# A state-space branch with its channels on partitions: tiled float32 products and scan rows in another order

## The chip, the cores and the metric

The kernel runs on one core of a Trainium2 chip. The metric is the device time of one execution in microseconds (us), taken as the median of three runs. The engines named below are TensorE (PE, with its weight loads PEld), VectorE (DVE), ScalarE (ACT), GpSimd (POOL) and SyncE (SP, which issues the DMAs here).

## What is computed

One residual block over 256 tokens of width 2048, in float32. One input projection feeds an mLSTM branch, a state-space branch (S5) and two gates; both branches are projected up, gated and added, then come an output projection and a SwiGLU network. The change concerns the S5 branch, which runs once:

```python
step = jnp.exp(log_step.astype(f32))[:, None]
a_bar = jnp.exp(lam * step)
b_bar = ((a_bar - 1.0) / lam)[..., None] * b_mat
ug = uf.reshape(bsz, s, S_GROUPS, S_GROUP).astype(jnp.complex64)   # 32 groups x 16 channels
bu = jnp.einsum('gpc,bsgc->bsgp', b_bar, ug)                       # 64 complex states per group
_, states = lax.associative_scan(linear_recurrence_combine, (a_seq, bu), axis=1)
y = jnp.einsum('gcp,bsgp->bsgc', c_mat, states).real.reshape(bsz, s, S_WIDTH)
y = y + d.astype(f32) * uf
y = jax.nn.gelu(y)
y = y * jax.nn.sigmoid(y @ w_glu.astype(f32) + b_glu.astype(f32))
```

## The kernel before

**The weight stream.** All weights arrive as 427 blocks of 128x1024 float32 on SP's DMA queue. ACT copies a block to `hi` in the rounded type float32r (L156), and DVE subtracts to get the rest `lo` (helper `TT`, L94). With both, each large product is done as three float32r products (`hi` with `hTh`, `lo` with `hTh`, `hi` with `hTl`): a block takes 12 matmuls of 512 columns on PE (`o2_block`, helper `mm`, L100). Three buffers of `hi` and `lo` let the splits run up to two blocks ahead of PE. The blocks come in the order of a table; chunk 4 of the input projection, which makes the S5 input `u`, is first (blocks 0 to 7), then the chunks of `x_m` and others.

**The two chains.** Between the blocks two Python generators are pumped, `s5_gen` for the S5 branch and `ml_gen` for the mLSTM branch. A generator emits a piece and yields its price for DVE and PE; `pump` spends a budget of each per block. A scheduler then reorders what was emitted, so the order on each engine is fixed before the run, and instructions of the chains stand between those of the blocks. The conv of the mLSTM branch is on DVE (`xcT`, `xml`).

**The S5 chain.** Two groups of 64 states fill the 128 partitions; there are 16 such pairs `j`. The input `u` has tokens on partitions (`s5ud`, 2 x 128x512). To bring it under the block-diagonal B, `u` and B are split into three float32r parts (`u`, `s5bd`), turned by products with the identity into `ust` and `bst` (96 rows deep), and 32 products of 256 columns make `bu`. `bu` holds, for each partition, [real or imaginary, pair `j`, token]. The scan runs inside 16 chunks of 16 tokens. Step `tau` makes, for all chunks at once, two products into `stm` (128x512: 2 x 16 pairs x 16 chunks), one addition to `bu` of 128x512 and two of 128x256; there are 15 steps. As a token's chunk is the outer index, a step reads one element, leaves 15 out, and reads the next. A recurrence over the chunks and a correction (`stm`, `bu`, 128x960) follow. Then 64 float32 products of 32 columns (the states as weights, block-diagonal C `cbd` in the tile `s5sp` moving) give `y` with tokens on partitions; after the gelu eight transposes on PE turn it to channels on partitions, in which the GLU product needs it.

Of the kernel before, what the change touches and what calls it, by code (L numbers as in the profile page):

```python
# [29 lines left out]
for _n, _w in (  # L30
    ("gmix", 16), ("g2", 16), ("cw", 32), ("cb", 8), ("mh", 8), ("skip", 8),
    ("bglu", 4), ("bif", 8), ("are", 16), ("aim", 16), ("ls", 16),
):
    PV[_n] = (_o, _o + _w)
    _o += _w
# [12 lines left out]
def block_kernel(ctx: ExitStack, tc: tile.TileContext, d, out):  # L48
# [56 lines left out]
    # ---------------------------------------------------------------- constants  # L105
# [19 lines left out]
    # ---------------------------------------------------------------- weight stream  # L125
# [114 lines left out]
    # ---------------------------------------------------------------- small helpers  # L240
# [29 lines left out]
    # ---------------------------------------------------------------- S5 chain  # L270
    s5 = {}

    def s5_gen():
# [5 lines left out]
        bd = [t2([P, 16, 32]) for _ in range(2)]  # L279
# [4 lines left out]
        nc.gpsimd.memset(bd[0], 0.0)  # L284
        nc.gpsimd.memset(bd[1], 0.0)
# [63 lines left out]
        while "bc" not in s5:  # L349
            yield 0  # L350
        bc = s5["bc"]
        bx = lambda a, n=16: a.unsqueeze(2).broadcast_to([P, 16, n])
        ta = m2([P, 16, 16])
        tb = m2([P, 16, 16])
        bdr = [u8([P, 16, 96], F32R, name="s5bd") for _ in range(2)]
        for ri in range(2):
            TT(ta, bc[:, 0 if ri == 0 else 1], bx(fr), MUL)
            TT(tb, bc[:, 1 if ri == 0 else 0], bx(fi), MUL)
            for g in range(2):
                ps_ = slice(g * 64, g * 64 + 64)  # L360
                TT(bd[ri][ps_, :, g * 16 : g * 16 + 16], ta[ps_], tb[ps_], SUB if ri == 0 else ADD)
            bv = bdr[ri].rearrange("p j (r c) -> p j r c", r=3)
            A.copy(bv[:, :, 0, :], bd[ri])
            A.copy(bv[:, :, 1, :], bd[ri])
            TT(bv[:, :, 2, :], bd[ri], f(bv[:, :, 0, :]), SUB)
            yield 1.8
        for g in range(2):
            ps_ = slice(g * 64, g * 64 + 64)
            cs = slice(g * 16, g * 16 + 16)
            V.tensor_copy(cbd[ps_, :, 0, cs], bc[ps_, 2])  # L370
            TS(cbd[ps_, :, 1, cs], bc[ps_, 3], -1.0)
        yield 1.0
        state["bd"] = 1
        yield 0.01, 0, 1
        # block-diagonal B, stacked (hi, hi, lo) along the contraction rows
        bst = [u8([P, 8, 2, 128], F32R, name="bst") for _ in range(2)]
        for jp in range(8):
            ps_ = aux()
            for jj in range(2):
                for ri in range(2):  # L380
                    c = (jj * 2 + ri) * 128
                    mm(ps_[0:96, c : c + 128], bdr[ri][:, 2 * jp + jj, :], identr, True, True)
            o = bst[jp // 4][:, 2 * (jp % 4) : 2 * (jp % 4) + 2].rearrange("p a b c -> p (a b c)")
            A.copy(o[0:96], ps_[0:96])
            yield 0.05, 0.45, (jp % 4) // 3
        state["bst"] = 1
        while "u" not in state:
            yield 0
        yield 0.01, 0, 2
        u3 = s5["u3"]  # L390
        bu = u32([P, 2, 16, 256], name="bu")
        usts = []
        for h in range(2):
            ust = u8([P, 8, 256], F32R, name="ust")
            usts.append(ust)
            for jp in range(4 * h, 4 * h + 4):
                ps_ = aux()
                for jj in range(2):
                    for tt in range(2):
                        c = (jj * 2 + tt) * 128  # L400
                        mm(ps_[0:96, c : c + 128], u3[tt][:, 2 * jp + jj, :], identr, True, True)
                o = ust[:, 2 * (jp % 4) : 2 * (jp % 4) + 2].rearrange("p a b -> p (a b)")
                A.copy(o[0:96], ps_[0:96])
                yield 0.05, 0.45, (jp % 4) // 3
        yield 0.01, 0, 1
        for h in range(2):
            ust = usts[h]
            for j in range(8 * h, 8 * h + 8):
                ps_ = aux()
                for ri in range(2):  # L410
                    mm(
                        ps_[:, ri * 256 : ri * 256 + 256],
                        bst[h][0:96, j % 8, ri, :],
                        ust[0:96, j % 8, :],
                        True,
                        True,
                    )
                A.copy(bu[:, :, j, :], ps_.rearrange("p (r t) -> p r t", r=2))
                yield 0.05, 0.25, (j % 3) // 2
        state["bu"] = 1  # L420
        # powers of a_bar: pw[:, ri, j, n] = a^(n+1)
# [18 lines left out]
        # scan inside chunks of 16  # L440
        X = bu.rearrange("p r j (c q) -> p r j c q", q=16)
        bc2 = lambda a: a.unsqueeze(1).unsqueeze(3).broadcast_to([P, 2, 16, 16])
        stm = u8([P, 2, 1024], name="stm")
        for tau in range(1, 16):
            pr = X[:, :, :, :, tau - 1]
            cu = X[:, :, :, :, tau]
            ta, tb = (stm[:, k, 0:512].rearrange("p (r j c) -> p r j c", r=2, j=16) for k in range(2))
            TT(ta, pr, bc2(ar), MUL)
            TT(tb, pr, bc2(ai), MUL)
            yield 1.2  # L450
            TT(cu, cu, ta, ADD)
            TT(cu[:, 0], cu[:, 0], tb[:, 1], SUB)
            TT(cu[:, 1], cu[:, 1], tb[:, 0], ADD)
            yield 1.3
        state["scan"] = 1
        # chunk-level recurrence
        for ri in range(2):
            V.tensor_copy(E[:, ri], X[:, ri, :, :, 15])
# [13 lines left out]
        # states: chunk-local + a^(tau+1) * state at the end of the chunk before; y = Re(C s) + D u, gelu  # L472
        ud = s5["ud"]

        def y_mm(jq, half):
            if half == 0:
                s5["yps"] = aux()
            ps_ = s5["yps"]
            for j in range(4 * jq + 2 * half, 4 * jq + 2 * half + 2):
                for tt in range(2):  # L480
                    c = tt * 256 + (j % 4) * 32
                    for ri in range(2):
                        mm(
                            ps_[:, c : c + 32],
                            bu[:, ri, j, tt * 128 : tt * 128 + 128],
                            cbd[:, j, ri, :],
                            ri == 0,
                            ri == 1,
                        )
            if half:  # L490
                pv_ = ps_.rearrange("p (a b) -> p a b", a=2)[:, :, 0:128]
                yv = ud[:, :, jq * 128 : jq * 128 + 128]
                TT(yv, pv_, yv, ADD)

        def gelu(h):
            y = ud[:, :, h * 256 : h * 256 + 256]
# [6 lines left out]
            A.activation(y, t, AF.Copy, scale=0.5)  # L503

        for jq in range(4):
            js = slice(4 * jq, 4 * jq + 4)
            sh = [P, 4, 15, 16]
            pb = [pw[:, ri, js, :].unsqueeze(2).broadcast_to(sh) for ri in range(2)]
            eb = [E[:, ri, js, 0:15].unsqueeze(3).broadcast_to(sh) for ri in range(2)]
            ta, tb = (stm[:, k, 0:960].rearrange("p (j c q) -> p j c q", j=4, c=15) for k in range(2))  # L510
            o = [X[:, ri, js, 1:16, :] for ri in range(2)]
            for ri in range(2):
# [6 lines left out]
                if jq and not ri:  # L519
                    y_mm(jq - 1, 0)  # L520
                    yield 0.05, 1.7
                    y_mm(jq - 1, 1)
                    yield 0.35, 1.7
# [5 lines left out]
        y_mm(3, 0)  # L529
        yield 0.05, 1.7  # L530
        y_mm(3, 1)
        yield 0.35, 1.7
        gelu(1)
        yield 1.9, 0, 1
        yt = u32([P, 2, 4, 256], name="yt")
        ygT = yt[:, 0]
        s5["sgt"] = yt[:, 1]
        ghl = u8([P, 2, 4, 256], F32R, name="ghl")
        gh, gl = ghl[:, 0], ghl[:, 1]
        for cpair in range(2):  # L540
            ps_ = aux()
            for cc in range(2):
                for tt in range(2):
                    ct = 2 * cpair + cc
                    c = (cc * 2 + tt) * 128
                    PE.transpose(ps_[:, c : c + 128], s5["ud"][:, tt, ct * 128 : ct * 128 + 128], ident)
            sl = slice(2 * cpair, 2 * cpair + 2)
            v2 = lambda a: a[:, sl, :].rearrange("p a b -> p (a b)")
            A.copy(v2(ygT), ps_)
            A.copy(v2(gh), v2(ygT))  # L550
            TT(v2(gl), v2(ygT), f(v2(gh)), SUB)
            yield 0.6, 0.45, 0
# [15 lines left out]
    # ---------------------------------------------------------------- mLSTM chain  # L568
    ml = {}

    def ml_gen():
# [93 lines left out]
        # log sigmoid of the forget gate  # L665
# [158 lines left out]
    # ---------------------------------------------------------------- main stream  # L824
# [9 lines left out]
    def win_evac(n, acc):  # L834
        if n == 4:
            u3 = u16([P, 2, 16, 96], F32R, name="u3")
            s5["u3"] = [u3[:, 0], u3[:, 1]]
            db = t2()
            nc.sync.dma_start(db, d["dbc"])
            ud = cp.tile([P, 2, 512], F32, name="s5ud")  # L840
            s5["ud"] = ud
            for tt in range(2):
                uf = ud[:, tt]
# [526 lines left out]
```

## Time and profile before

| what | value |
|---|---|
| median of 3 runs | 1292.4 us (1292.08 to 1292.52) |
| span of the profiled execution, first to last instruction | 1291.1 us |
| PE busy | 1264.4 us, 98% |
| DVE busy | 808.5 us, 63% |
| ACT busy | 611.8 us, 47% |
| chain that ended last | PE 85%, DVE 11%, issue 2% |

The profiled execution has no time of its own beside its span; 1.3 us lie between the span and the median. Busy is an average over the whole span: PE is near its full span, and DVE has three tenths free overall, but not in each stretch.

### The profile page before, as it was taken

The page shows a single profiled execution, that of the slowest core. Times are in us where ns is not written, and L with a number is a line of the kernel's source. Part 1 is how long each engine was busy: PE and PEld are TensorE (multiplying, and loading weights), DVE is VectorE, ACT ScalarE, POOL GpSimd, SP SyncE. Part 2 cuts the span into 40 slices and gives each one's busy share as a digit, 9 for nine tenths or more (in the row PEclk, how much of TensorE's full clock was granted, in tenths as well). Part 3 has the DMA queues.
Part 4 walks back from the last instruction along what each step waited for, and adds up shares of the span by engine and source line. Part 5 has one row for each costly group of instructions (what it writes and reads, how often), then busy time and mean ns, then how long its engine had stood idle before and what let it go on. Part 6 is the DMA issues. An engine that isn't in the chain of part 4 may idle for free.

```text
span 1291.1 us, 15585 instructions
## 1 busy us (share of the span) xinstructions
PE 1264.4 (98%) x5932; PEld 1053.8 (82%) x5932; DVE 808.5 (63%) x1127; ACT 611.8 (47%) x768; POOL 2.1 (0%) x8
## 2 busy tenths in 40 slices
PE   7999989999999999999999999999999999999997
PEld 5888877888888888888888888888888888888885
DVE  8848996899958665565555545555555554545544
ACT  6777533354655445454444444444444433434443
POOL 0000000000000000000000000000000000000000
PEclk9999998999999999999999999999999999999999
DMA  7655445444445576665556665455655666666454
GB/s 273 209 167 171 159 146 166 161 159 136 147 145 174 183 246 191 241 226 186 194 190 186 188 193 188 147 170 189 205 186 163 208 240 195 201 188 203 151 164 145
DMA packets 66874, 238.23 MB, mean 185 GB/s; under 512 B 7408, under 2 KB 8176, under 8 KB 66544
## 3 DMA queue, kind: packets, MB, share of 16 engines
q1 hardware_dynamic: 66800, 237.25, 56.5%
q8 instruction: 46, 0.75, 0.2%
q14 instruction: 28, 0.23, 0.1%
HBM read 235.12 MB, written 2.10 MB: 184 GB/s over the span
## 4 chain that ended last, share of the span: by engine, by line
PE 85%; DVE 11%; issue 2%; ACT 1%; DMA 0%; SPq 0%; ACTq 0%; DVEq 0%
PE acc L100 80%; PE aux L100 4%; DVE lo L94 3%; DVE bu L94 2%; DVE stm L94 2%; PE aux L1097 1%; DVE s5sp L94 0%; DMA raw<-in_w_in_dram 0%; ACT hi L156 0%; DVE hTl L97 0%; DVE xcT L97 0%; DVE m L97 0%; PE aux L1036 0%; PE aux L1000 0%; PE aux L808 0%
## 5 line engine op out<-in xcount | busy, mean ns | idle before, releaser
L94 DVE TENSOR_TENSOR lo<-raw,hi 128x1024 fp32r<-128x1024 f32 x427 | 522.9, 1225 | 427.9 <-ACT hi L156 425.9
L156 ACT CAST hi<-raw 128x1024 fp32r<-128x1024 f32 x427 | 449.4, 1053 | 598.9 <-PE acc L100 522.7
L100 PE MATMUL acc<-lo,h2h 128*128 128x512 f32 x704 | 275.0, 391 | 0.0
L100 PE MATMUL acc<-hi,h2l 128*128 128x512 f32 x704 | 274.0, 389 | 0.0
L100 PE MATMUL acc<-hi,h2h 128*128 128x512 f32 x704 | 249.9, 391 | 0.0
L100 PE MATMUL acc<-hi,aT 128*128 128x512 f32 x664 | 204.9, 389 | 0.0
L100 PE MATMUL acc<-lo,hTh 128*128 128x512 f32 x416 | 168.4, 405 | 5.7 <-DVE lo L94 5.5
L100 PE MATMUL acc<-hi,hTl 128*128 128x512 f32 x416 | 165.2, 397 | 0.0
L100 PE MATMUL acc<-hi,hTh 128*128 128x512 f32 x416 | 154.6, 399 | 9.3 <-ACT hi L156 9.3
L100 PEld LDWEIGHTS acc<-hi,h2h 128*128 128x128 f32 x704 | 132.1, 188 | 27.2
L100 PEld LDWEIGHTS acc<-lo,h2h 128*128 128x128 f32 x704 | 132.1, 188 | 27.1
L100 PEld LDWEIGHTS acc<-hi,h2l 128*128 128x128 f32 x704 | 132.2, 188 | 27.1
L100 PEld LDWEIGHTS acc<-hi,aT 128*128 128x128 f32 x664 | 124.6, 188 | 25.8
L100 PE MATMUL acc<-lo,aT 128*128 128x512 f32 x332 | 129.2, 389 | 0.0
L100 PEld LDWEIGHTS acc<-hi,hTh 128*128 128x128 f32 x416 | 78.8, 191 | 25.6 <-ACT hi L156 9.7
L100 PEld LDWEIGHTS acc<-lo,hTh 128*128 128x128 f32 x416 | 79.6, 191 | 24.7 <-DVE lo L94 9.3
L100 PEld LDWEIGHTS acc<-hi,hTl 128*128 128x128 f32 x416 | 79.5, 191 | 15.5
L100 PEld LDWEIGHTS acc<-lo,aT 128*128 128x128 f32 x332 | 62.3, 188 | 12.9
L94 DVE TENSOR_TENSOR bu<-bu,stm 128x256 f32<-128x256 f32 (+2 forms) x61 | 52.4, 881 | 0.1
L100 PE MATMUL acc<-lo,mTh 128*128 128x512 f32 x128 | 50.2, 392 | 0.0
L100 PE MATMUL acc<-hi,mTl 128*128 128x512 f32 x128 | 49.8, 389 | 0.0
L100 PE MATMUL acc<-hi,mTh 128*128 128x512 f32 x128 | 46.0, 391 | 0.0
(251 smaller groups left out, 982.5 us busy)
## 6 DMA issues: line engine op xcount, KB each, us to landing
raw<-in_w_in_dram SPq DMA_DIRECT2D x104, 512.0 KB, 3.6
raw<-in_w_ffn_gate_dram SPq DMA_DIRECT2D x88, 512.0 KB, 3.5
raw<-in_w_ffn_up_dram SPq DMA_DIRECT2D x88, 512.0 KB, 3.5
raw<-in_w_ffn_down_dram SPq DMA_DIRECT2D x88, 512.0 KB, 4.3
raw<-in_w_out_dram SPq DMA_DIRECT2D x32, 512.0 KB, 3.6
raw<-in_w_up_m_dram SPq DMA_DIRECT2D x16, 512.0 KB, 3.9
raw<-in_w_up_s_dram SPq DMA_DIRECT2D x8, 512.0 KB, 3.5
t<-in_bg_dram SPq DMA_DIRECT2D x8, 256.0 KB, 3.5
```

The costliest lines, as they stand in the source:

```text
L94: return V.tensor_tensor(o, a, b, op=op)
L100: return PE.matmul(o, l, r, start=start, stop=stop, skip_group_check=True)
L156: A.copy(hi, raw)
L1097: PE.transpose(ps_[:, (cc * 2 + tt) * 128 : (cc * 2 + tt) * 128 + 128], av[tt][:, ct * 128 : ct * 128 + 128], ident,)
```

## The change

Chunk 4 is multiplied the other way round, with the weights stationary and the tokens moving, so that `u` leaves PE with channels on partitions; its eight blocks take 192 products of 256 columns instead of 96 of 512. Its evacuation multiplies by the reciprocal norm of a token, which is now needed along the columns: a product with ones spreads it over the partitions (`r1b`). `u` goes straight into tiled float32 products: B in the tile `s5bT` is taken 32 rows at a time as weights, each with 32 channel rows of `u`, and the four strips of rows write four PSUM tiles. The identity products, the splits of `u` and B, `bst` and `ust` are gone. Per token order, `bu` is now [position in chunk, chunk], so that a scan step reads rows of 16 neighbours. The products with C take `cbd` as weights, 32 columns wide, and write 32 PSUM rows each, so that `y` is made with channels on partitions; the eight transposes and the copies behind them are gone. The factor of the ZOH step is applied to C and not to B, D u is added in the evacuation of `y`, and the last copy of the gelu puts the tokens back in order. Two constants are loaded ahead of their old place and one is gone; the first blocks' DMA queue has 0.5 MB more on it.

```diff
-        for h in range(2):
-            ust = usts[h]
-            for j in range(8 * h, 8 * h + 8):
-                ps_ = aux()
-                for ri in range(2):
-                    mm(
-                        ps_[:, ri * 256 : ri * 256 + 256],
-                        bst[h][0:96, j % 8, ri, :],
-                        ust[0:96, j % 8, :],
...
+        for ct in range(4):
+            pss = [aux() for _ in range(4)]
+            for ri in range(2):
+                for jj in range(4):
+                    rs = slice(32 * jj, 32 * jj + 32)
+                    mm(pss[jj][:, ri * 256 : ri * 256 + 256], bT[rs, ct, ri, :], uT[rs, ct, :], True, True)
+            for jj in range(4):
+                A.copy(bu[:, :, 4 * ct + jj, :], pss[jj].rearrange("p (r t) -> p r t", r=2))
+            yield 0.05, 1.3, 1
...
-        X = bu.rearrange("p r j (c q) -> p r j c q", q=16)
+
+        X = bu.rearrange("p r j (q c) -> p r j q c", c=16)
...
-            pr = X[:, :, :, :, tau - 1]
-            cu = X[:, :, :, :, tau]
+            pr = X[:, :, :, tau - 1, :]
+            cu = X[:, :, :, tau, :]
...
+        def y_mm(jq):
+            ps_ = aux()
+            for ri in range(2):
+                for jj in range(4):
+                    j = 4 * jq + jj
+                    mm(ps_[32 * jj : 32 * jj + 32, 0:256], cbd[:, j, ri, :], bu[:, ri, j, :], ri == 0, ri == 1)
+            STT(ud[:, jq, :], ud[:, jq, :], pvs("s5d", jq), ps_[:, 0:256], MUL, ADD)
...
+            rb = s5["r1b"].rearrange("p (q c) -> p q c", c=16).unsqueeze(1).broadcast_to([P, 2, 16, 16])
+            for h in range(2):
+                o = ud[:, 2 * h : 2 * h + 2, :].rearrange("p a (q c) -> p a q c", c=16)
+                TT(o, acc[h].rearrange("p (a c q) -> p a q c", a=2, q=16), rb, MUL)
...
+                for ct in range(4):
+                    mm(o_(ct), w_(hi, ct), xh, kt == 0 and ct % 2 == 0, False)
+                    mm(o_(ct), w_(hi, ct), xl, False, False)
+                for ct in range(4):
+                    mm(o_(ct), w_(lo, ct), xh, False, kt == 15 and ct % 2 == 1)
```

On PE, where the states' input is made, the kernel before has these rows; `aux` is a PSUM tile, and `x2` is the real and the imaginary product of one pair.

```order
L100 MATMUL acc_683<-hi_804,hTh_77 128x512
L100 MATMUL aux_838<-ust_734,bst_606 128x256 x2
L100 MATMUL acc_683<-lo_805,hTh_77 128x512
L100 MATMUL acc_683<-hi_804,hTl_79 128x512
L100 MATMUL aux_842<-ust_734,bst_606 128x256 x2
```

In the changed kernel the second of its four sets of tiled products stands in the stream like this; aux_701, 702, 703 and 704 are the strips of rows 0, 32, 64 and 96.

```order
L100 MATMUL acc_761<-hi_685,hTh_76 128x512
L100 MATMUL aux_701<-s5ud,s5bT_400 128x256
L100 MATMUL aux_702<-s5ud,s5bT_400 128x256
L100 MATMUL aux_701<-s5ud,s5bT_400 128x256
L100 MATMUL aux_703<-s5ud,s5bT_400 128x256
L100 MATMUL aux_704<-s5ud,s5bT_400 128x256
L100 MATMUL aux_702<-s5ud,s5bT_400 128x256
L100 MATMUL aux_703<-s5ud,s5bT_400 128x256
L100 MATMUL aux_704<-s5ud,s5bT_400 128x256
L100 MATMUL acc_761<-lo_686,hTh_76 128x512
```

The eight products of a set stand as neighbours, mostly on different strips, between two products of the stream that use the whole array.

On DVE, the scan of the kernel before stands among the splits `lo` like this; one step is `stm` x2, `bu` of 512 and `bu` of 256 x2.

```order
L94 TENSOR_TENSOR stm_1428<-bu_733,s5sm 128x512 x2
L94 TENSOR_TENSOR bu_733<-bu_733,stm_1428 128x512
L94 TENSOR_TENSOR lo_1503<-raw_1408,hi_1502 128x1024
L94 TENSOR_TENSOR bu_733<-bu_733,stm_1428 128x256 x2
L94 TENSOR_TENSOR stm_1428<-bu_733,s5sm 128x512 x2
L94 TENSOR_TENSOR bu_733<-bu_733,stm_1428 128x512
L94 TENSOR_TENSOR lo_1535<-raw_1431,hi_1534 128x1024
```

In the changed kernel the scan begins at block 20 instead of block 42; these rows are at blocks 25 to 27 (`lo_934` is the split of block 25).

```order
L94 TENSOR_TENSOR lo_934<-raw_874,hi_933 128x1024
L97 SCALAR_TENSOR_TENSOR xcT_1016<-xmT_1015,pv,xcT_1016 128x254 x2
L94 TENSOR_TENSOR stm_928<-bu_666,s5sm 128x512 x2
L94 TENSOR_TENSOR lo_957<-raw_892,hi_956 128x1024
L94 TENSOR_TENSOR xcT_1016<-xcT_1016,m_1570 128x512
L97 SCALAR_TENSOR_TENSOR xcT_1016<-xmT_1015,pv,xcT_1016 128x255 x2
L94 TENSOR_TENSOR bu_666<-bu_666,stm_928 128x32x16
L94 TENSOR_TENSOR lo_979<-raw_910,hi_978 128x1024
L94 TENSOR_TENSOR xml_1227<-xmT_1015,xmh_1226 128x1024
L97 SCALAR_TENSOR_TENSOR xcT_1016<-xmT_1015,pv,xcT_1016 128x253 x4
L94 TENSOR_TENSOR bu_666<-bu_666,stm_928 128x16x16 x2
L94 TENSOR_TENSOR xml_1227<-xmT_1015,xmh_1226 128x1024
```

The scan's rows have moved to where the conv of the mLSTM branch also stands, and out of the later blocks.

## Rows read from the trace of the kernel before

**Rows 1.** Page, busy time and the chain that ended last, by engine.
```profile
PE 1264.4 (98%) x5932; PEld 1053.8 (82%) x5932; DVE 808.5 (63%) x1127; ACT 611.8 (47%) x768; POOL 2.1 (0%) x8
...
PE 85%; DVE 11%; issue 2%; ACT 1%; DMA 0%; SPq 0%; ACTq 0%; DVEq 0%
```

**Rows 2.** PE timeline, 166 to 209 us: start, length, instruction, idle before and releaser.
```profile
166.19 0.50 PE L100 MATMUL acc<-lo,hTh 128*128 128x512 f32 x1 [1.19 <-DVE lo L94]
...
171.29 0.38 PE L100 MATMUL aux<-xch,lo 128*128 128x256 f32 x1 [2.05 <-DVE lo L94]
...
175.53 0.38 PE L100 MATMUL aux<-xch,lo 128*128 128x256 f32 x1 [1.11 <-DVE lo L94]
...
202.07 0.79 PE L100 MATMUL acc<-lo,hTh 128*128 128x512 f32 x1 [3.09 <-DVE lo L94]
...
203.09 0.63 PE L100 MATMUL acc<-lo,hTh 128*128 128x512 f32 x1
203.52 0.63 PE L100 MATMUL acc<-hi,hTl 128*128 128x512 f32 x1
...
208.19 0.39 PE L100 MATMUL acc<-lo,hTh 128*128 128x512 f32 x1
```

**Rows 3.** Windows: length, busy time of PE, PEld, DVE, ACT, POOL, granted clock, DMA.
```profile
180.00:202.00 22.00, 18.98 (x97) 15.59 (x95) 21.86 (x26) 7.96 (x9) 0.00 (x0) 0.98 0.48 144
202.00:209.00 7.00, 6.92 (x18) 5.47 (x19) 4.50 (x6) 1.04 (x1) 0.00 (x0) 0.56 0.67 219
```

**Rows 4.** Chain of waits in order of time: start, length, instructions.
```profile
60.39 1.34 PE aux L100 x16
...
134.22 5.75 PE aux L100 x48
...
329.44 1.71 PE aux L100 x16
...
603.62 43.34 PE acc L100 x191
```

**Rows 5.** Groups of instructions on PE, by form: busy time, mean ns.
```profile
L100 PE MATMUL aux<-s5sp,bu 128*128 128x32 f32 x128 | 15.3, 267 | 0.0
L100 PE MATMUL aux<-ust,bst 96*128 96x256 f32 x32 | 5.9, 285 | 0.0
...
L100 PE MATMUL aux<-identr,u 128*96 128x128 f32 x32 | 3.1, 246 | 0.0
```

**Rows 6.** PE timeline, 313 to 317 us: float32 products.
```profile
313.93 2.75 PE L100 MATMUL aux<-vk,m 128*128 128x256 f32 x12
316.51 0.75 PE L100 MATMUL aux<-s5sp,bu 128*128 128x32 f32 x6
```

**Rows 7.** Groups of instructions on DVE, by form.
```profile
L94 DVE TENSOR_TENSOR stm<-bu,s5sm 128x512 f32<-128x512 f32 x30 | 30.0, 1042 | 0.3
...
L94 DVE TENSOR_TENSOR bu<-bu,stm 128x256 f32<-128x256 f32 x30 | 17.2, 619 | 0.1
L94 DVE TENSOR_TENSOR bu<-bu,stm 128x512 f32<-128x512 f32 x15 | 16.4, 1091 | 0.0
...
L94 DVE TENSOR_TENSOR xcT<-xcT,m 128x512 f32<-128x512 f32 x4 | 2.8, 690 | 0.9 <-ACT m L646 0.9
...
L94 DVE TENSOR_TENSOR m<-s5bc,s5sm 128x256 f32<-128x256 f32 x4 | 1.6, 421 | 0.0
```

**Rows 8.** DVE timeline, 106 to 110 us, in the conv.
```profile
106.43 0.48 DVE L97 SCALAR_TENSOR_TENSOR xcT<-xmT,pv,xcT 128x255 f32<-128x255 f32 x1
106.82 0.69 DVE L94 TENSOR_TENSOR xcT<-xcT,m 128x512 f32<-128x512 f32 x1
107.42 0.48 DVE L97 SCALAR_TENSOR_TENSOR xcT<-xmT,pv,xcT 128x255 f32<-128x255 f32 x1
107.82 1.22 DVE L94 TENSOR_TENSOR xml<-xmT,xmh 128x1024 fp32r<-128x1024 f32 x1
108.95 1.23 DVE L94 TENSOR_TENSOR lo<-raw,hi 128x1024 fp32r<-128x1024 f32 x1
```

More of the change, by code (lines that the diff above doesn't have):

```diff
@@ L31 @@
     ("gmix", 16), ("g2", 16), ("cw", 32), ("cb", 8), ("mh", 8), ("skip", 8),
-    ("bglu", 4), ("bif", 8), ("are", 16), ("aim", 16), ("ls", 16),
+    ("bglu", 4), ("s5d", 4), ("bif", 8), ("are", 16), ("aim", 16), ("ls", 16),
 ):
@@ L278, in s5_gen @@
         ar, ai, fr, fi, am1, inv = (sv(i) for i in range(13, 19))
-        bd = [t2([P, 16, 32]) for _ in range(2)]
         sp = u8([P, 2048], name="s5sp")
@@ L283, in s5_gen @@
         cbd = sp[:, 1024:2048].rearrange("p (a b c) -> p a b c", a=16, b=2)
-        nc.gpsimd.memset(bd[0], 0.0)
-        nc.gpsimd.memset(bd[1], 0.0)
         nc.gpsimd.memset(cbd, 0.0)
@@ L348, in s5_gen @@
         yield 1.0
-        while "bc" not in s5:
+        while "cc" not in s5:
             yield 0
-        bc = s5["bc"]
-        bx = lambda a, n=16: a.unsqueeze(2).broadcast_to([P, 16, n])
+        cc_ = s5["cc"]
+        bx = lambda a: a.unsqueeze(2).broadcast_to([P, 16, 16])
         ta = m2([P, 16, 16])
         tb = m2([P, 16, 16])
-        bdr = [u8([P, 16, 96], F32R, name="s5bd") for _ in range(2)]
         for ri in range(2):
-            TT(ta, bc[:, 0 if ri == 0 else 1], bx(fr), MUL)
-            TT(tb, bc[:, 1 if ri == 0 else 0], bx(fi), MUL)
+            TT(ta, cc_[:, ri], bx(fr), MUL)
+            TT(tb, cc_[:, 1 - ri], bx(fi), MUL)
@@ L359, in s5_gen @@
             for g in range(2):
                 ps_ = slice(g * 64, g * 64 + 64)
[L361 to L377, printed above, removed]
-            ps_ = aux()
-            for jj in range(2):
-                for ri in range(2):
[L381 to L385, printed above, removed]
@@ L386, in s5_gen @@
-        state["bst"] = 1
+                o = cbd[ps_, :, ri, g * 16 : g * 16 + 16]
+                if ri == 0:
+                    TT(o, ta[ps_], tb[ps_], SUB)
+                else:
+                    STT(o, ta[ps_], -1.0, tb[ps_], MUL, SUB)
+            yield 1.6
+        state["cbd"] = 1
         while "u" not in state:
             yield 0
-        yield 0.01, 0, 2
-        u3 = s5["u3"]
+        yield 0.01, 0, 1
+        uT = s5["ud"]
+        bT = s5["bT"]
         bu = u32([P, 2, 16, 256], name="bu")
-        usts = []
@@ L393, in s5_gen @@
-        for h in range(2):
[L394 to L404, printed above, removed]
@@ L405, in s5_gen @@
-        yield 0.01, 0, 1
-        for h in range(2):
-            ust = usts[h]
-            for j in range(8 * h, 8 * h + 8):
-                ps_ = aux()
-                for ri in range(2):
-                    mm(
-                        ps_[:, ri * 256 : ri * 256 + 256],
-                        bst[h][0:96, j % 8, ri, :],
-                        ust[0:96, j % 8, :],
[L415 to L419, printed above, removed]
+        for ct in range(4):
[7 more added lines that the diff above has]
+            yield 0.05, 1.3, 1
@@ L457, in s5_gen @@
         for ri in range(2):
-            V.tensor_copy(E[:, ri], X[:, ri, :, :, 15])
+            V.tensor_copy(E[:, ri], X[:, ri, :, 15, :])
         ta, tb = (stm[:, k, 0:32].rearrange("p (r j) -> p r j", r=2) for k in range(2))
@@ L473, in s5_gen @@
         ud = s5["ud"]
[L475 to L493, printed above, removed]
+        def y_mm(jq):
[5 more added lines that the diff above has]
+            STT(ud[:, jq, :], ud[:, jq, :], pvs("s5d", jq), ps_[:, 0:256], MUL, ADD)
         def gelu(h):
-            y = ud[:, :, h * 256 : h * 256 + 256]
+            y = ud[:, 2 * h : 2 * h + 2, :]
             t = t2().rearrange("p (a b) -> p a b", a=2)
@@ L502, in gelu @@
             STT(t, t, 1.0, y, ADD, MUL)
-            A.activation(y, t, AF.Copy, scale=0.5)
+            A.activation(
+                y.rearrange("p a (c q) -> p a c q", q=16),
+                t.rearrange("p a (q c) -> p a c q", c=16),
+                AF.Copy,
+                scale=0.5,
+            )
         for jq in range(4):
             js = slice(4 * jq, 4 * jq + 4)
[L507 to L511, printed above, removed]
+            sh = [P, 4, 16, 15]
+            pb = [pw[:, ri, js, :].unsqueeze(3).broadcast_to(sh) for ri in range(2)]
+            eb = [E[:, ri, js, 0:15].unsqueeze(2).broadcast_to(sh) for ri in range(2)]
+            ta, tb = (stm[:, k, 0:960].rearrange("p (j q c) -> p j q c", j=4, c=15) for k in range(2))
+            o = [X[:, ri, js, :, 1:16] for ri in range(2)]
             for ri in range(2):
@@ L519, in s5_gen @@
                 if jq and not ri:
[L520 to L523, printed above, removed]
+                    y_mm(jq - 1)
+                    yield 0.45, 1.3
             if jq == 2:
@@ L528, in s5_gen @@
         yield 0.01, 0, 1
[L529 to L532, printed above, removed]
+        y_mm(3)
+        yield 0.45, 1.3
         gelu(1)
         yield 1.9, 0, 1
-        yt = u32([P, 2, 4, 256], name="yt")
-        ygT = yt[:, 0]
-        s5["sgt"] = yt[:, 1]
+        ygT = ud
+        s5["sgt"] = u8([P, 4, 256], name="sgt")
         ghl = u8([P, 2, 4, 256], F32R, name="ghl")
         gh, gl = ghl[:, 0], ghl[:, 1]
[L540 to L549, printed above, removed]
+        for hh in range(2):
+            v2 = lambda a: a[:, 2 * hh : 2 * hh + 2, :].rearrange("p a b -> p (a b)")
             A.copy(v2(gh), v2(ygT))
             TT(v2(gl), v2(ygT), f(v2(gh)), SUB)
-            yield 0.6, 0.45, 0
+            yield 0.7
         s5["yg"] = (ygT, gh, gl)
@@ L835, in win_evac @@
         if n == 4:
[L836 to L840, printed above, removed]
-            s5["ud"] = ud
-            for tt in range(2):
-                uf = ud[:, tt]
-                A.activation(uf, acc[tt], AF.Copy, scale=r1[:, tt : tt + 1])
-                uv = uf.rearrange("p (j c) -> p j c", c=32)
-                o = s5["u3"][tt].rearrange("p j (r c) -> p j r c", r=3)
-                A.copy(o[:, :, 0, :], uv)
-                A.copy(o[:, :, 2, :], uv)
-                TT(o[:, :, 1, :], uv, f(o[:, :, 0, :]), SUB)
-                TT(uf, uf, db, MUL)
+            ud = cp.tile([P, 4, 256], F32, name="s5ud")
+            s5["ud"] = ud
+            rb = s5["r1b"].rearrange("p (q c) -> p q c", c=16).unsqueeze(1).broadcast_to([P, 2, 16, 16])
+            for h in range(2):
+                o = ud[:, 2 * h : 2 * h + 2, :].rearrange("p a (q c) -> p a q c", c=16)
+                TT(o, acc[h].rearrange("p (a c q) -> p a q c", a=2, q=16), rb, MUL)
             state["u"] = 1
@@ L893, in win_mm @@
             cur["acc"] = [acc_tile(), acc_tile()]
-        o2_block(cur["acc"], lhs_h, (2 * kp, 2 * kp + 1), hi, lo, kp == 0, kp == 7)
+        if n == 4:
+            for q in range(2):
+                kt = 2 * kp + q
+                xh, xl = hTh[kt // 8][:, kt % 8, :], hTl[kt // 8][:, kt % 8, :]
+                w_ = lambda a, ct: a[:, q * 512 + ct * 128 : q * 512 + ct * 128 + 128]
+                o_ = lambda ct: cur["acc"][ct // 2][:, (ct % 2) * 256 : (ct % 2) * 256 + 256]
+                for ct in range(4):
[3 more added lines that the diff above has]
+                    mm(o_(ct), w_(lo, ct), xh, False, kt == 15 and ct % 2 == 1)
+        else:
+            o2_block(cur["acc"], lhs_h, (2 * kp, 2 * kp + 1), hi, lo, kp == 0, kp == 7)
         if kp == 7:
@@ L1246, in rms1 @@
         rstd(r1, s1, "r1")
+        dg = m2([P, 256])
+        for tt in range(2):
+            TS(dg[:, tt * 128 : tt * 128 + 128], ident, r1[:, tt : tt + 1])
+        pb = aux()
+        mm(pb[:, 0:256], ones[:, 0:128], dg, True, True)
+        s5["r1b"] = cp.tile([P, 256], F32, name="r1b")
+        A.copy(
+            s5["r1b"].rearrange("p (q c) -> p q c", c=16), pb[:, 0:256].rearrange("p (c q) -> p q c", q=16)
+        )
     s5g = Gen(s5_gen())
@@ L1265, in block_kernel @@
             if i == 1:
-                s5["bc"] = u8([P, 4, 16, 16], name="s5bc")
-                nc.sync.dma_start(s5["bc"], d["s5bc"])
+                s5["cc"] = m2([P, 2, 16, 16], name="s5c")
+                nc.sync.dma_start(s5["cc"], d["s5c"])
             if i == 3:
@@ L1273, in block_kernel @@
                 nc.sync.dma_start(wif, d["wif"])
+                s5["bT"] = u8([P, 4, 2, 128], name="s5bT")
+                nc.sync.dma_start(s5["bT"], d["s5bT"])
         if i + SL < 8:
@@ L1323, in _layout @@
         "cb": col(g["conv_b"][0]), "mh": col(g["mh_norm_g"][0]), "skip": col(g["skip"][0]),
-        "bglu": col(g["b_glu"][0]), "bif": np.broadcast_to(g["b_if"][0], (128, 8)),
+        "bglu": col(g["b_glu"][0]), "s5d": col(g["s5_d"][0]), "bif": np.broadcast_to(g["b_if"][0], (128, 8)),
         "are": par(g["s5_a_re"][0]), "aim": par(g["s5_a_im"][0]), "ls": ls,
@@ L1327, in _layout @@
     a["pv"] = c(np.concatenate([cols[n] for n in PV], axis=1))
-    bre, bim = (g[n][0].reshape(16, 2, 64, 16).transpose(1, 2, 0, 3).reshape(128, 1, 16, 16) for n in ("s5_b_re", "s5_b_im"))
-    cre, cim = (g[n][0].reshape(16, 2, 16, 64).transpose(1, 3, 0, 2).reshape(128, 1, 16, 16) for n in ("s5_c_re", "s5_c_im"))
-    a["s5bc"] = c(np.concatenate([bre, bim, cre, cim], axis=1))
-    a["dbc"] = c(np.broadcast_to(g["s5_d"][0], (128, 512)))
+    a["s5c"] = c(
+        np.stack([g[n][0].reshape(16, 2, 16, 64).transpose(1, 3, 0, 2).reshape(128, 16, 16) for n in ("s5_c_re", "s5_c_im")], axis=1)
+    )
+    bT = np.zeros((4, 2, 16, 4, 2, 2, 64), f32)
+    for k, n in enumerate(("s5_b_re", "s5_b_im")):
+        b_ = g[n][0].reshape(4, 4, 2, 64, 16)
+        for e in range(2):
+            bT[:, e, :, :, k, e, :] = b_[:, :, e].transpose(1, 3, 0, 2)
+    a["s5bT"] = bT.reshape(128, 4, 2, 128)
     a["bg"] = c(np.broadcast_to(g["b_gate"][0], (128, 4096)))
```

## The prediction

> **What bounds the kernel now.** I read the page first, then the chain of waits, then the timeline of PE where the chain leaves it. PE is busy 98% of the span and carries 85% of the chain [rows 1]: what PE no longer has to do is gained, what it is given in addition is lost, and work of ACT and DVE counts only where PE waits for it. One stretch is of that kind. In the stretch up to 202 us the chain runs over DVE, which splits blocks and scans in turn: from 180 to 202 it is busy 21.86 of 22 us, PE only 18.98 [rows 3]. PE's timeline there has four gaps that a `lo` ends, 1.19, 2.05, 1.11 and 3.09 us, in sum 7.44 [rows 2]. After the longest the clock is lower: 0.56 granted from 202 to 209 us [rows 3], and matmuls start 0.43 us apart instead of 0.227 [rows 2, 4]. That is the 1.2 GHz level for about 6 us; before it PE had stood idle for 3.09 us, while the shorter gaps were followed by no fall. From 202.07 to 208.19 us I count 14 products of 512 columns; at full speed they take 3.2 us, so the fall cost 2.9.
>
> **Prices on PE.** A float32r product of 512 columns takes 43.34/191 = 0.227 us, one of 256 columns 5.75/48 = 0.120, an identity product 1.34/16 = 0.084, a product of `y` in float32 with 32 columns 1.71/16 = 0.107 per instruction [rows 4]. A float32 product of 256 columns is (316.51 - 313.93)/12 = 0.215 per instruction [rows 6]; the trace records two instructions for each float32 product (64 products of `y` in the code, 128 in the trace [rows 5]), so one costs 0.43.
>
> **What is removed on PE.** 32 identity products of `u` and as many of B at 0.084: 5.4. 32 products of `ust` and `bst` at 0.120: 3.8. 128 instructions of `y` at 0.107: 13.7. Eight transposes at the identity price: 0.7. Sum 23.6 [rows 4, 5].
>
> **What is added on PE.** Chunk 4: 192 x 0.120 - 96 x 0.227 = 1.2; it lies among the start's waits, so it may cost nothing. The product that spreads `r1b`: 0.4. The tiled products: 32 for `bu` and 32 for `y`, 256 columns each, 128 instructions at 0.215, if one runs at a time: 27.5. The trace has no product on a part of the array, so this is the unknown price. One at a time is the upper end, 27.5; all four strips at once is the lower, 6.9. I take two at once, 13.8, nearer the lower end: the two instructions of one product use the same strip and stand one behind the other, so the second has to follow the first, while the next product's first can run beside it on its own strip. The order bears this out: the neighbours are mostly strips of different rows, with a strip named twice in a row at places.
>
> The Trainium skill, "TensorE: Matmul & The Clock Gate", section "Measured speedup vs the span model", gives 3.07 times for four row strips (K=32, 512 columns); an estimate from it would be 27.5/3.07 = 9.0 and the total 4.8 us lower than mine. It says nothing of float32 in two instructions, and no row here shows it.
>
> **Switches between tiled and full products.** By the order the tiled products stand in six groups for `bu` and six for `y`, each with a full product ahead and behind: 24 switches. No row shows one. The lower bound is nothing; the upper is the length of a product beyond its pitch, the drain of what is under way: 0.39 recorded [rows 2] less 0.227, 0.16 each, 3.9 in all. I take the middle, 2.0.
>
> Net on PE: -23.6 + 1.2 + 0.4 + 13.8 + 2.0 = **-6.2**, from -16.3 (four at once, chunk 4 hidden, no cost of a switch) to +9.4.
>
> **The scan.** A step before: 2 x 1.042 + 1.091 + 2 x 0.619 = 4.41 us of DVE; an element taken every 16th place is what these rows share [rows 7]. On dense rows of the same length DVE takes 0.690 (512) and 0.421 (256) [rows 7], so a step becomes 2 x 0.690 + 0.690 + 2 x 0.421 = 2.91. Fifteen steps give back 22.5 us of DVE. That is no time by itself; it is worth the stalls. The order shows that the scan moved from blocks 42 on to blocks 20 to 49: where the four gaps lay only light steps are left, and I take all of **-7.4**, and with the 3.09 gap the fall of the clock, **-2.9**.
>
> What is late next: the conv. In the changed kernel three scan steps stand in the nine blocks 24 to 32 beside it. Their pitch on DVE, from one start to the next, is 0.40 for a conv step, 0.60 for its product, 1.13 for `xml` and `lo` [rows 8]; scan rows likewise 0.09 below their lengths. By the order: 9 `lo` 10.2, 24 conv steps 9.6, 3 products 1.8, 2 `xml` 2.3, scan 6 x 0.60 + 3 x 0.60 + 7 x 0.33 = 7.7; together 31.6. PE has 9 blocks x 12 x 0.227 = 24.5 and eight transposes, 0.9. DVE is 6.2 too long; the lead of up to two blocks (2 x 2.72 = 5.4) covers part. With a full lead PE stands 0.8 us, with none 6.2; I take **+3.0**. It is several gaps of the size that were followed by no fall in [rows 2].
>
> **At no cost.** ACT loses the copies of `bst`, `ust`, `u` and the transposes, and keeps 16 of `bu`; it is busy 47% [rows 1]. The three constants on SP ahead of the first blocks add 0.5 MB; the blocks are loaded ahead of their casts, so this is hidden, and if not costs about 1 us once. PE now waits for DVE at the `r1b` product and the evacuation of `u`; queued behind are blocks whose halves are already split, so I count nothing; without that cover it is one evacuation, under 1 us. The chain of the second gelu keeps its place before the GLU product, so I leave PE's wait there as it is.
>
> **The sum.** -6.2 - 7.4 - 2.9 + 3.0 = -13.5: span 1291.1 - 13.5 = 1277.6. The median lay 1.3 above the profiled span, so I say **1279** for the median.
>
> **The rivals.**
> - *Four strips at once.* The strips share nothing in rows 32 apart, and each `bu` strip has a PSUM tile of its own. Against it: each product is two instructions on one strip, in order. 6.9 lower: **1272**.
> - *The stalls come back with the clock.* For it: 6.2 us of excess in the conv. If the lead is nothing and a gap reaches 3 us, +3.2 and +2.9: **1285**. Against it: gaps of 1 to 2 us were followed by no fall [rows 2], and DVE catches up between.
> - *Each switch drains the array.* Price 0.16 as above, +1.9: **1281**. The Trainium skill, "TensorEngine Tiling (Array Packing)", section "Key Properties", states that a change of tiling mode drains TensorE; no row here shows it, and by that rule the time would be this.
> - *One at a time.* The tiling then saves nothing on PE: +13.7, **1293**, no change. For it: no row shows an overlap of two products. 64 products cancel all gains at 27.3 us, or 0.213 per instruction, which is just the price in [rows 6].
> - *Slower: one at a time, with the weights loaded in between.* An instruction of `y` costs 0.107 with 32 columns [rows 4], more than its columns: that is the floor of loading a new set of weights. If that load cannot run beside the strip before it, an instruction costs 0.215 + 0.107 = 0.32, 41 us in all: +27, **1306**. It decides for slower by over 0.2% from 0.234 per instruction. Against it: full products hide their loads behind the product before.
>
> **How the numbers follow.** Two at once 0.48 (its own range, from the bounds of stall and switch: 1273 to 1284), four at once 0.20, the stalls and the clock 0.11, drains 0.07, one at a time 0.09, loads in between 0.05. The range 1268 to 1290 leaves out the last two, 0.14, and reaches below four at once by the switches' and chunk 4's lower ends. A change under 0.2% (2.6 us) can't be told from none. Faster holds the first four, 0.86, and a little of the fifth: 0.87; same 0.08; slower 0.05.
>
> **What would show it.** PE's timeline at `aux` from `s5ud`, `s5bT`: starts 0.1 apart for two at once, 0.05 for four, 0.2 for one. The same for 32x256 rows of `y`. On DVE `stm` of 128x512 at 0.69 and `bu` at 0.69 and 0.42. No gap at blocks 42 to 58, no half clock there; gaps of 1 to 2 us with `lo` as releaser at blocks 25 to 33. What would make it wrong most: the price of a tiled product, or a gap long enough for the clock to fall again.

## The result and the profile after

The changed kernel takes 1271.1 us (median of 4 runs, 1269.6 to 1271.7) against 1292.2 of the kernel before: ratio 0.9834, 95% interval 0.982 to 0.9849, 21 us faster. The profiled span went from 1291.1 to 1269.9 us. The prediction had 1279 and a range that holds the result; the direction was right, the gain was 1.6 times the forecast.

The page of the changed kernel, in the parts of [rows 1]:

```profile
PE 1252.2 (99%) x5926; PEld 1040.6 (82%) x5926; DVE 784.1 (62%) x1121; ACT 600.0 (47%) x741; POOL 1.2 (0%) x6
...
PE 98%; ACT 1%; DVE 0%; DMA 0%; issue 0%; SPq 0%; ACTq 0%; DVEq 0%
```

DVE held 11% of the chain and now holds none. PE's waits, by releaser (us in total, times, longest), of the changed kernel:

```profile
PE acc L100 <- ACT hi L156: 7.2, 1, 7.2
PE acc L100 <- DVE lo L94: 1.8, 1, 1.8
```

The four gaps of [rows 2] are gone, and so is one of 1.2 us that the kernel before had in the gelu. One new gap stands where the prediction put it, in the conv, with `lo` as releaser. The clock fell behind it: 0.54 is granted from 100.60 to 104.10 us, which is the 1.2 GHz level. PE's timeline there (start, length, instruction, idle before):

```profile
98.24 0.61 PE L100 MATMUL acc<-hi,hTh 128*128 128x512 f32 x2
100.66 0.65 PE L100 MATMUL acc<-lo,hTh 128*128 128x512 f32 x1 [1.81 <-DVE lo L94]
101.11 0.63 PE L100 MATMUL acc<-hi,hTl 128*128 128x512 f32 x1
101.54 0.63 PE L100 MATMUL acc<-lo,hTh 128*128 128x512 f32 x1
```

From 101 to 104 us products start 0.43 us apart, as in [rows 2] after 202 us; that costs 1.6 us beside the gap.

The tiled products, PE's timeline of the changed kernel, first one set of `bu` (eight products, 16 instructions), then one of `y`, each between two products of the stream:

```profile
53.05 0.39 PE L100 MATMUL acc<-hi,hTl 128*128 128x512 f32 x1
53.37 1.15 PE L100 MATMUL aux<-s5ud,s5bT 32*128 32x256 f32 x16
54.44 0.50 PE L100 MATMUL acc<-hi,hTh 128*128 128x512 f32 x1
54.78 0.39 PE L100 MATMUL acc<-lo,hTh 128*128 128x512 f32 x1
...
62.33 1.13 PE L100 MATMUL aux<-s5ud,s5bT 32*128 32x256 f32 x4
...
64.05 1.15 PE L100 MATMUL aux<-s5ud,s5bT 32*128 32x256 f32 x12
...
322.99 1.07 PE L100 MATMUL aux<-bu,s5sp 128*32 128x256 f32 x16
323.99 0.50 PE L100 MATMUL acc<-lo,hTh 128*128 128x512 f32 x1
```

Sixteen instructions take 54.44 - 53.37 = 1.07 us; at 0.215 one at a time they would take 3.44 and two at a time 1.72. So all four strips run at once: four steps of 0.216. The single records of the trace say the same: four starts within 21 ns, then the next four. A broken set is worth less: four instructions on one strip (62.33) take as long as sixteen on four. Around a set the neighbours are stretched: 53.05 to 53.37 and 54.44 to 54.78 are 0.32 and 0.34 instead of 0.227, and 1.07 is 0.21 more than four steps. A group so costs about 0.41 us beside its steps for `bu`, and by the same sum 0.33 for `y`.

DVE in the changed kernel, groups by form, in answer to [rows 7]:

```profile
L94 DVE TENSOR_TENSOR stm<-bu,s5sm 128x512 f32<-128x512 f32 x30 | 19.4, 683 | 3.1 <-ACT bu L378 3.0
...
L94 DVE TENSOR_TENSOR bu<-bu,stm 128x256 f32<-128x256 f32 x30 | 11.3, 415 | 0.1
L94 DVE TENSOR_TENSOR bu<-bu,stm 128x512 f32<-128x512 f32 x15 | 10.2, 681 | 0.0
```

A scan step costs 2 x 0.683 + 0.681 + 2 x 0.415 = 2.88 us instead of 4.41.

### The profile page after: what moved, and what is told of

Read it like the earlier page. It is cut to its first block, busy times and chain, and to the rows that moved or that the text cites. A ratio compares the mean times of both kernels' runs of the same rounds, so it can differ in the third digit from the quotient of the medians.

```text
span 1269.9 us, 15534 instructions
## 1 busy us (share of the span) xinstructions
PE 1252.2 (99%) x5926; PEld 1040.6 (82%) x5926; DVE 784.1 (62%) x1121; ACT 600.0 (47%) x741; POOL 1.2 (0%) x6
## 4 chain that ended last, share of the span: by engine, by line
PE 98%; ACT 1%; DVE 0%; DMA 0%; issue 0%; SPq 0%; ACTq 0%; DVEq 0%
PE acc L100 91%; PE aux L100 5%; PE aux L1043 1%; DMA raw<-in_w_in_dram 0%; ACT hi L156 0%; PE aux L982 0%; PE aux L749 0%; PE aux L946 0%; PE aux L558 0%; ACT xcT L531 0%; DVE xcT L97 0%; PE aux L709 0%; DVE lo L94 0%; ACT xmT L527 0%; ACT xmh L541 0%
## 5 line engine op out<-in xcount | busy, mean ns | idle before, releaser
L100 PE MATMUL acc<-lo,hTh 128*128 128x512 f32 x384 | 154.3, 402 | 1.8 <-DVE lo L94 1.8
L100 PE MATMUL acc<-hi,hTl 128*128 128x512 f32 x384 | 151.8, 395 | 0.0
L100 PE MATMUL acc<-hi,hTh 128*128 128x512 f32 x384 | 141.5, 397 | 0.0
L100 PEld LDWEIGHTS acc<-lo,hTh 128*128 128x128 f32 x384 | 72.9, 190 | 19.5 <-DVE lo L94 2.5
L100 PEld LDWEIGHTS acc<-hi,hTh 128*128 128x128 f32 x384 | 72.6, 190 | 16.3 <-issue 1.0
L100 PEld LDWEIGHTS acc<-hi,hTl 128*128 128x128 f32 x384 | 73.0, 190 | 15.1 <-issue 0.3
L94 DVE TENSOR_TENSOR bu<-bu,stm 128x256 f32<-128x256 f32 (+2 forms) x61 | 40.0, 673 | 0.1
```

What stands on the lines that cost most here:

```text
L94: return V.tensor_tensor(o, a, b, op=op)
L100: return PE.matmul(o, l, r, start=start, stop=stop, skip_group_check=True)
```

## The experiments

**The order of the tokens, taken back in the changed kernel.** All else stays.

```diff
-        X = bu.rearrange("p r j (q c) -> p r j q c", c=16)
+        X = bu.rearrange("p r j (c q) -> p r j q c", q=16)
...
-                o = ud[:, 2 * h : 2 * h + 2, :].rearrange("p a (q c) -> p a q c", c=16)
-                TT(o, acc[h].rearrange("p (a c q) -> p a q c", a=2, q=16), rb, MUL)
+                TT(ud[:, 2 * h : 2 * h + 2, :], acc[h].rearrange("p (a b) -> p a b", a=2), rb, MUL)
```

> The changed kernel with the tokens of bu back in the order [chunk, position], all else kept: tiled products, channels on partitions. Theory A (the dense rows free DVE, and that is what removes the waits for lo): a scan step costs 4.4 us of DVE again instead of 2.9, the steps now stand beside the conv, three of them add 4.5 us of waits in blocks 23 to 32, and the steps behind them bring back the 7.4 us of gaps and the 2.9 us of lower clock of the kernel before: about 1286, span 15 us above the changed kernel's 1269.9. Rival B (the gain is PE's alone, the order of the tokens only moves work that is hidden): 1271, within 1 us of the changed kernel. In the trace stm of 128x512 is back at 1.04 us in either case.

Measured: 1282.6 us, 11.4 above the changed kernel's 1271.1 (the sum had 15). One row of DVE by form, then PE's waits and its longest gap:

```profile
L94 DVE TENSOR_TENSOR stm<-bu,s5sm 128x512 f32<-128x512 f32 x30 | 30.1, 1043 | 3.1 <-ACT bu L378 3.0
```

```profile
PE acc L100 <- DVE lo L94: 9.5, 8, 3.0
...
PE aux L100 <- DVE lo L94: 0.4, 2, 0.2
```

Waits for `lo` rise from 1.8 to 9.9 us. Of these 6.6 lie in the conv (88 to 107 us), 4.8 more than in the changed kernel, where the sum had 4.5. Behind it only 3.3 came back where the sum had 7.4, and the clock fell twice, as often as in the changed kernel; so the sum was too high. Rival B falls: the order of the tokens is worth half of the gain.

**The order of the tokens alone, in the kernel before.** The products stay as they were.

```diff
-                A.copy(bu[:, :, j, :], ps_.rearrange("p (r t) -> p r t", r=2))
+                for ri in range(2):
+                    A.copy(
+                        bu[:, ri, j, :].rearrange("p (q c) -> p q c", c=16),
+                        ps_[:, ri * 256 : ri * 256 + 256].rearrange("p (c q) -> p q c", q=16),
+                    )
...
-        X = bu.rearrange("p r j (c q) -> p r j c q", q=16)
+        X = bu.rearrange("p r j (q c) -> p r j q c", c=16)
```

> The kernel before with only the order of the tokens in bu changed to [position, chunk]; the copies that fill bu turn the order (two of 256 instead of one of 512 on ACT). y keeps that order from its products on and D u is added in the other order, so that the order of the tokens in the S5 branch's output is left undone. Theory A: stm at 0.69 us, the four gaps of 7.4 us and the 2.9 us of lower clock at 202 us are gone, all products on PE stay: 1282. Rival B: 1292, no change. If both A and the sum of parts hold, this and the run with the old order in the changed kernel bracket the 21 us: about 10 from the order, the rest from PE's products.

Measured: 1281.0 us against 1292.1 on the same chip, ratio 0.9911 (0.9896 to 0.9926): 11.1 us faster, the sum had 10. The scan stands where it stood; PE waits for `lo` 1.1 us in all, and behind the first products, which start at half clock in every run, no stretch of half clock is left.

```profile
PE acc L100 <- ACT hi L156: 8.3, 2, 7.1
PE acc L100 <- DVE lo L94: 1.1, 3, 0.6
```

The two runs bracket it: about 11 us from the order of the tokens, about 10 from the products of PE.

**The tiled products on the whole array.** Each instruction now uses all rows and columns; the number and length of the instructions stay.

```diff
-                    mm(pss[jj][:, ri * 256 : ri * 256 + 256], bT[rs, ct, ri, :], uT[rs, ct, :], True, True)
+                    mm(pss[jj][:, ri * 256 : ri * 256 + 256], bT[:, ct, ri, :], uT[:, ct, :], True, True)
...
-                    mm(ps_[32 * jj : 32 * jj + 32, 0:256], cbd[:, j, ri, :], bu[:, ri, j, :], ri == 0, ri == 1)
+                    w = 1024 + 128 * ((2 * j + ri) % 8)
+                    mm(ps_[:, 0:256], sp[:, w : w + 128], bu[:, ri, j, :], ri == 0 and jj == 0, ri == 1 and jj == 3)
```

> The changed kernel with its 64 tiled products on the whole array: B with all 128 rows at once and C with 128 columns, the same number and length of products (their sums mix channels, so u and y are not the reference's). Theory A (four strips run at once, 42 steps of 0.216 us, and a change between tiled and full costs 0.37 us in and out, 12 times): 13.5 us of tiled work become 128 x 0.215 = 27.5, +14: 1285. Rival (strips run two at once, and the gain over the forecast is elsewhere): the tiled work was about 18 and the difference is +10 or less: 1281 or less. By one at a time nothing changes: 1271.

Measured: 1283.9 us, 12.8 above 1271.1. A set on PE's timeline now takes 56.81 - 53.54 = 3.27 us instead of 1.07:

```profile
53.54 3.61 PE L100 MATMUL aux<-s5ud,s5bT 128*128 128x256 f32 x16
56.81 0.58 PE L100 MATMUL acc<-hi,hTh 128*128 128x512 f32 x1
```

In this run the gap in the conv is 1.19 us and no fall of the clock follows it, 2.2 us less than in the changed kernel, and PE waits 0.7 us more in chunk 4. With both counted the products themselves cost some 14 us more, as the sum had. The tiling is worth more than PE's whole share of the gain: on the whole array 128 steps of 0.216 us are 27.6 us, more than the 23.6 that were removed.

**Each tiled product for `bu` twice.**

```diff
-            for ri in range(2):
+            for ri in (0, 1, 0, 1):
                 for jj in range(4):
```

> The changed kernel with each of the 32 tiled products for bu issued twice (the second writes the same PSUM rows with the same values). By the order the four sets then stand whole, 16 products each, in four groups instead of six. Theory A (four at once, 0.216 us a step, 0.37 a pair of changes): 32 steps and 4 groups, 8.4 us, instead of 24 steps and 6 groups, 7.4: +1.0, 1272. Rival, two at once: 32 more products at 0.216 less two groups: +6, 1277. One at a time: +13.

Measured: 1274.5 us, 3.4 above the changed kernel, where the sum had 1; the span is 1271.4, 1.5 above. One at a time (1284) falls. The time lies halfway between the sum's 1272 and the 1277 of two at once and does not decide between them; the length of a set does. A set of 32 instructions takes 1.94 us, eight steps and 0.21, where two at once would need sixteen steps, 3.5 us:

```profile
53.36 2.01 PE L100 MATMUL aux<-s5ud,s5bT 32*128 32x256 f32 x32
55.30 0.50 PE L100 MATMUL acc<-hi,hTh 128*128 128x512 f32 x1
```

Part of the rest is waits for `lo`: 2.9 us instead of 1.8. Against that, this profile lacks the fall of the clock that the changed kernel has at 186 us (see the next run), some 1.7 us. About 1 us of the span's difference, and more of the medians', stays unexplained; the runs of each kernel scatter over 2 us.

**The changed kernel again, beside the next three.**

> The changed kernel again, for the runs beside it: 1271. If the gap of 1.8 us in the conv and the lower clock behind it are the order's doing, both are there again at about 100 us. If the other fall of the clock, at 186 us behind 24 products of 8 columns without a gap, is chance, it can be absent.

Measured: 1271.4 us. The gap of 1.81 us is there at 101.0, and the second fall of the clock too, at 186.9 us. That fall has no gap ahead of it. PE's timeline of this run:

```profile
182.94 2.74 PE L100 MATMUL aux<-wif,qT 128*128 128x8 f32 x24
185.53 0.49 PE L100 MATMUL acc<-hi,hTh 128*128 128x512 f32 x1
...
186.91 0.63 PE L100 MATMUL acc<-hi,hTl 128*128 128x512 f32 x1
187.34 0.63 PE L100 MATMUL acc<-hi,hTh 128*128 128x512 f32 x1
```

**The scan late, the sets whole.**

```diff
-            yield 0.05, 1.3, 1
+            yield 0.05, 1.3, 3
         state["bu"] = 1
```

> The changed kernel with three blocks instead of one between two sets of tiled products; by the order the four sets then stand whole, the conv is done by block 35, and the scan stands at blocks 42 to 58, where it was before the change. Theory A (conv and scan beside each other make the gap; a broken set costs eight steps instead of four): the gap of 1.8 us and the 1.8 us of lower clock are gone, the tiled products for bu take 16 steps and 4 groups, 4.9 us instead of 7.4: 1265. Rival (the scan makes a gap wherever it stands, or is late for y and the GLU product): 1270 or more.

Measured: 1269.9 us (1269.0 to 1271.3), not 1265. Both halves of theory A hold up to 340 us: there is no gap in conv or scan, and from 110 to 180 us the run is 6 us ahead of the changed kernel (gap 1.8, fall 1.6, sets 2.5). From 190 us it is 7.7 ahead, since the second fall is absent too, which theory A did not claim. Then the rival takes 5 us back. PE's waits and, at the end of the GLU, its timeline:

```profile
PE acc L100 <- ACT ghl L503: 3.1, 1, 3.1
PE acc L100 <- DVE lo L94: 0.7, 1, 0.7
...
368.69 0.50 PE L100 MATMUL acc<-hi,ghl 128*128 128x512 f32 x1 [3.14 <-ACT ghl L503]
...
369.42 0.63 PE L100 MATMUL acc<-hi,ghl 128*128 128x512 f32 x1
```

With the late scan `y` is late, and the S5 branch's up-projection waits 3.1 us for its input; the clock falls behind that, which costs another 1.6 us.

**Two products of a strip behind each other.**

```diff
-            for ri in range(2):
-                for jj in range(4):
+            for jj in range(4):
+                for ri in range(2):
```

> The changed kernel with the two products of a strip of rows issued one behind the other (four instructions on one strip, then four on the next); by the order the sets then stand whole. If a strip takes its instructions whenever it is free, whatever stands ahead of them for other strips, a set is four steps of 0.216 us with all strips in each: 4.9 us for bu instead of 7.4, 1268 to 1269, with the gap in the conv still there. If instructions start strictly in the order in which they are issued, as my prediction had it, the next strip can start only with the last of the four ahead: 13 steps a set, +28 steps over the changed kernel: about 1277.

Measured: 1269.6 us (1266.3 to 1272.0). Now four instructions on one strip stand ahead of the first of the next, and still a set takes 1.09 us:

```profile
53.18 1.17 PE L100 MATMUL aux<-s5ud,s5bT 32*128 32x256 f32 x16
54.27 0.50 PE L100 MATMUL acc<-hi,hTh 128*128 128x512 f32 x1
```

By the single records the first four starts are 13 to 14 ns apart. The records name no strip, but one strip alone takes 0.216 us from one start to the next (the four instructions at 62.33 above), so these are four strips. So a strip does not wait for what stands ahead on another. This decides between the two readings: the one of my prediction asked for 13 steps, 2.8 us a set. The gap in the conv stays, 2.2 us here; in the profiled execution (1266.3) no fall of the clock follows it. The other three executions of this kernel take 3.3 to 5.7 us longer at a lower mean granted clock (0.994 and 0.995 against 0.998), so the clock probably fell in them; no trace of them was kept.

**Pairs, and the scan's first step later.**

```diff
-        yield 0.01, 0, L2
+        yield 0.01, 0, 16
```

> The pairs of the run beside it, and 16 blocks instead of 4 between the set-up of the scan and its first step; by the order it begins at block 27 instead of 20, and the conv stands mostly ahead of it. If A holds, DVE still has five steps beside the last conv blocks, so that a gap under 1 us may stay: 1265 to 1268. Rival: the gap moves with the scan, 1268 as without the delay.

Measured: 1265.4 us (1265.4 to 1265.9), ratio 0.9792 (0.9779 to 0.9806) to the kernel before; its interval lies below that of the changed kernel in the same set of runs, 0.9836 (0.9823 to 0.985). The sets of `bu` are whole, PE's waits are

```profile
PE acc L100 <- ACT hi L156: 6.9, 1, 6.9
PE acc L100 <- DVE lo L94: 1.3, 2, 0.7
```

and behind the first products no stretch of half clock is left. The rival falls: of the gap in the conv 0.6 us is left, at 99.6 us. This version is 6 us faster than the changed kernel, of the size of its gap (1.8), the two falls (1.6 and 1.7) and the broken sets (2.5) less what it still waits.

## Why the prediction was right, and where it was off

The span fell by 21.2 us, the sum had 13.5. The time lies inside the stated range, but below the 1273 to 1284 that went with two strips at once: the range held because it took in the rival, not because the price was right.

- **The scan** was right. The step was forecast at 2.91 us and is 2.88; the gaps of 7.4 us and the fall of 2.9 are gone. The run with the order alone measured 11.1 us for a forecast of 10.3.
- **The price of a tiled product** is the step that failed: "the second has to follow the first, while the next product's first can run beside it". The second does follow the first, but the next strips do not wait for their turn behind it. The run with pairs shows it. It is 42 steps of 0.216, 9.1 us, not 13.8; the steps are more than the 32 of whole sets because the scheduler broke two sets of `bu` and the groups of `y`. The rival with four strips named the mechanism and 1272. That the time came within 1 us of it is partly luck: its steps and switches, 6.9 + 2.0, measured 13.6, and gains that it did not have made up for that (1.2 behind the old groups of `y`, 1.1 in chunk 4, 1.2 in the gelu, 1.0 of short waits; all below).
- **The switches** were too cheap: 2.0 taken, 3.9 as the upper bound, 4.5 measured (six groups at 0.41 and six at 0.33). The product after the group is late as well as the one ahead. That a change of tiling mode drains TensorE, as the Trainium skill has it ("TensorEngine Tiling (Array Packing)", section "Key Properties"), agrees with the stretched starts. But the late product behind the group is not due to tiling alone: in the kernel before, the product behind a group of `y` stands 0.32 us ahead of its next one too, with no tile in sight:

```profile
316.51 0.75 PE L100 MATMUL aux<-s5sp,bu 128*128 128x32 f32 x6
317.10 0.48 PE L100 MATMUL acc<-lo,hTh 128*128 128x512 f32 x1
317.42 0.39 PE L100 MATMUL acc<-hi,hTl 128*128 128x512 f32 x1
```

  The kernel before had 13 such groups of `y`; their 1.2 us were missing from what is removed. Steps and switches together are 13.6 us where 15.8 were forecast.
- **Chunk 4** costs 0.1 us, not 1.2: its 96 products take 25.4 us before (8.03 to 33.48) and its 192 products 25.5 after (7.24 to 33.24, less two products of block 8 that stand between them). PE waited 0.34 us for a `lo` there before and does not after; what else hides the difference was not separated.
- **The gap in the conv** was right in place and cause. Its size is near by luck: 3.0 was all idle time and stood for 1.8 of idle time and 1.6 of lower clock. The argument that "gaps of 1 to 2 us were followed by no fall" did not carry over: one of 1.81 us was followed by a fall here.
- **Held to stay, or left out**: the prediction left PE's wait in the second gelu as it is. That wait, 1.2 us for a cast that stands behind the gelu and its copies on ACT, is gone with the transposes and copies (a gain); with the order of the tokens alone it stayed (1.22 us at 365 us). Three shorter waits for `lo`, 1.0 us in all, at 115, 272 and 311 us of the kernel before, are gone too. The fall at 186 us is a loss of 1.7. The wait in the kernel before:

```profile
379.00 0.73 PE L100 MATMUL acc<-hi,hTh 128*128 128x512 f32 x2 [1.22 <-ACT hi L156]
```

- **Not settled**: some 3 us of the 21.2. PE starts 0.8 earlier in this execution; first products lie between 6.9 and 7.6 us in the later runs, and at 8.0 in the profile before, so I take this for scatter. Some 2 us are spread over many small differences that no experiment separated.

## What to carry to other kernels

Where DVE is full in one stretch, the order of elements in a tile is worth looking at: a step over every 16th element cost 4.4 us and a dense one 2.9, and that alone was 11 us. Products that use 32 rows or 32 columns are cheap only in whole sets with all four strips in them, since a group costs 0.3 to 0.4 us beside its steps and one strip alone as much time as four. When work moves to an earlier place, look at what stands there already, and at who waits for its end: the scan beside the conv cost 3.4 us (1.8 of wait, 1.6 of lower clock), and the late scan 4.7 at the GLU (3.1 and 1.6).

## What the runs showed of the hardware

- Four strips of the array run independently: sixteen float32 instructions of 256 columns take four steps of 0.216 us, in each order of issue that was tried, and sixteen steps on the whole array. From the first of the set to the next product that is 1.07 us against 3.27, 3.1 times. With the delay of the neighbours on both sides counted (0.09 and 0.11 around a set; 0.19 behind the sixteen on the whole array) it is 1.28 against 3.46, 2.7 times. The Trainium skill, "TensorE: Matmul & The Clock Gate", section "Measured speedup vs the span model", has 3.07 for four row strips; what this case measures lies on either side of it, by what is counted.
- The Trainium skill, "TensorE: Matmul & The Clock Gate", section "The mechanism", says that matmuls keep their order in start and end. In the run with pairs, instructions of the next strip start before earlier ones of the first; if the order in which the instructions reach the engine is that of the program, this differs, and the measurement decides.
- The clock fell to half at 186 us of the changed kernel (0.51 granted from 186.20 to 189.70 us) with PE busy all the time, right behind 24 products of 8 columns (2.74 us), in both profiles of this kernel, and behind the same row in the run on the whole array (at 191.8 us). In the profiles of three other runs (old order, each product twice, pairs) the same row of 24 stands with no fall behind it; in the run with pairs products start 0.23 us apart there:

```profile
178.83 2.74 PE L100 MATMUL aux<-wif,qT 128*128 128x8 f32 x24
181.42 0.49 PE L100 MATMUL acc<-hi,hTh 128*128 128x512 f32 x1
...
182.91 0.40 PE L100 MATMUL acc<-hi,hTh 128*128 128x512 f32 x1
183.14 0.39 PE L100 MATMUL acc<-lo,hTh 128*128 128x512 f32 x1
```

  And the length of a gap does not decide alone: 1.81 us was followed by a fall, 2.05 [rows 2] and 2.2 in the run with pairs were not. What decides stays open.
